# Two edits to a two-layer attention trunk: the mixing ratio of projections and attention in its second layer, and the position bias of the compression on Pool and DVE

## The chip, the cores and the metric

The kernel runs on one core of a Trainium2 chip. Its engines are TensorE (PE; its weight loads are listed as PEld), VectorE (DVE), ScalarE (ACT) and GpSimd (POOL); SyncE (SP) issues the DMAs. The metric is the device time of one execution in microseconds, taken as the median of several runs. In the rows, L1265 is line 1265 of the kernel before; busy times are in us.

## What is computed

Two layers over 1024 tokens of width 1024, in float32. The first has an attention with the 256 best keys for each query (a) and a sliding-window attention (b). The second, with which the change deals, has a three-part attention (c) and a latent attention (d). Cut to what matters:

```python
def nsa_compress(z, pe, w1, w2):                 # keys and values of (c), blocks of 32 tokens, step 16
    ch = z.reshape(bsz, seq // 16, 16, 2, 64)
    blocks = concatenate([ch[:, :-1], ch[:, 1:]], axis=2) + pe[None, None, :, None, :]
    flat = blocks.transpose(0, 1, 3, 2, 4).reshape(bsz, 63, 2, 32 * 64)
    return silu(flat @ w1) @ w2                  # w1: 2048 x 128

def layer_cd(x, ...):
    y = rms_norm(x, norm_g) @ w_in               # all projections: qc kc vc ks vs kw vw gc zc cq ckv kr zd
    kc, vc = nsa_compress(kc, ...), nsa_compress(vc, ...)
    oc = nsa_attention(...)                      # compressed keys + all keys of blocks + window of 512
    q  = rms_norm(cq) @ d_w_uq                   # 8 heads x (64 + 32)
    kv = rms_norm(ckv) @ d_w_ukv                 # 8 heads x (64 keys + 64 values)
    od = mla_attention(...)                      # causal over all keys
    return x + concatenate([oc * silu(zc), od * silu(zd)]) @ w_out
```

Because the bias `pe` is added ahead of the linear map, `(z + pe) @ w1` is `z @ w1` plus one vector of 128 numbers for the keys and one for the values.

## The kernel before

The tokens lie in 8 tiles of 128. Every projection is a chunk of up to 280 columns (`chunk`, `fill_gen`, L480 to L543): for each tile it accumulates 8 x 3 matmuls in a bank of PSUM (`pp`, two banks; weights and input are split into a high and a low part, so three products) and hands the bank to a `post` function, which copies it out and mostly posts a chain of further steps (norm, rotation, transposes through the three buffers of `psT`).

The order is written by a planner, `Lanes`. A main generator (the attention) and a fill generator (the projections) yield costs in planner units; after each main step, `Lanes.run` (L153) takes fill steps until the fill's sum reaches `ratio` times the main's sum. A unit of scores costs heads x 2 x max(107, 0.42 x keys), a block of transposes 110 and a block of value products 87 for each 128x128; a quarter of a projection tile costs 6 x max(107, 0.42 x columns). Posted chains advance by one step with each of these steps. The result is a program order; the framework then places each engine's instructions by a timeline of its own in which the program order is the priority, so that an instruction that is ready may go ahead of earlier ones that wait, as far as buffers allow; buffers of a pool come in program order.

Layer two runs as follows. `FO` holds the last projection of layer one and then the chunks `ks kc kw qc0 zc0 zc1 cq qc1 zd0 zd1 ck` (FOO, L57). When `kc` is through, `compress()` (L1254) is posted: for keys (n = 0) and then values (n = 1) it forms the bias, as 16 matmuls of one column against the 16 slices of `w1` (L1265), then the hidden layer (L1276) and the second map (L1291). When the first queries are there, `L.run(attn_gen(c_jobs(0) + c_jobs(1)), FC, CR)` (L1792) runs the three-part attention: for each half of the heads (g) eight query tiles in the order CO, each as compressed, full and window unit. It is filled with the rest of `FO` and behind it `d_prologue` (L1616): it closes the pool of projection weights, opens the one of the last attention in the same space, loads and splits that attention's weights (`small_w`), makes the keys of its first four heads (`d_keys`, eight tiles in pairs) and up to two queries (`next_query`). The chunk `cq` is held back until the first half of the heads is done (`gate`, L1485), since it takes the buffers of that half's keys. What of the fill is left when the attention has been planned, up to the last keys, follows at L1793. Then the values of the last attention are made (L1802; their buffers are those of the three-part attention's values), and the last attention runs with its own fill, `d_fill`, and with `wout_gen`, which loads and splits the output weights. The chunk `ck` (keys' latent) is 160 columns wide; its chain ends with the copy `krs` (L1465).

Names in rows: `pt` probabilities, `hp`/`ht` their transposed halves, `hl` their split for a transposing DMA, `po` the values' sum, `kcs` the compressed keys, `qs` queries, `kd`, `qhl`, `qrs` keys and queries of the last attention, `whq`, `whkv` its weights, `rs_y` reciprocal roots, `gnope` its gains.

Of the kernel before, what the change touches and what calls it, by code (L numbers as in the profile page):

```python
# [10 lines left out]
F32 = mybir.dt.float32  # L11
# [7 lines left out]
OP = mybir.AluOpType  # L19
AX = mybir.AxisListType  # L20
PSUM = bass.MemoryType.PSUM

P = 128
# [21 lines left out]
QB = 3  # L45
TR = 1.4
TA = 0.65
CR = 0.88
DR = 0.8
WB = 2  # L50
WP = 2
# [19 lines left out]
PTB = 3  # L71
# [113 lines left out]
def trunk(ctx: ExitStack, tc: tile.TileContext, A, out):  # L185
    nc = tc.nc
    V, S, G, T = nc.vector, nc.scalar, nc.gpsimd, nc.tensor
# [4 lines left out]
    wk = ctx.enter_context(tc.tile_pool(name="wk", bufs=2))  # L192
# [25 lines left out]
    half = cst.tile([P, 16], F32, name="half")  # L218
# [140 lines left out]
    def tps():  # L359
        return psT.tile([P, 4, P], F32, name="psT")  # L360
# [727 lines left out]
    for c in tk:  # L1088
        m += c
        L.tick()  # L1090
        while f < TR * m and c is not None:
            c = next(FA)
# [161 lines left out]
    def compress():  # L1254
        for n in range(2):
            w1 = B["w1"][n]
            zT = B["zT"][n]
            pe = cp.tile([P, 16], F32, name="pe")
            nc.sync.dma_start(pe, A["c_cmp_pe"][0, n].rearrange("(a b) d -> (b d) a", b=2))
            w2 = cp.tile([P, 64], F32, name="w2")  # L1260
            nc.sync.dma_start(w2, A["c_cmp_w2"][0, n])
            yield from L.take_in("psT", PTC)
            ph = tps().rearrange("p a n -> p (a n)")
            for a in range(16):
                T.matmul(ph[:, 0:1], w1[:, a], pe[:, a:a + 1], start=a == 0, stop=a == 15)  # L1265
            bias = cp.tile([P, 2], F32, name="bias", bufs=2)
            V.tensor_copy(bias[:, 0:1], ph[:, 0:1])
            L.give("psT")
            V.tensor_scalar(bias[:, 1:2], bias[:, 0:1], 0.5, None, op0=OP.mult)
            yield  # L1270
# [4 lines left out]
            for a in range(16):  # L1275
                T.matmul(p2[:, :, 0:NCMP], w1[:, a], zT[:, :, 2 * a:2 * a + 16 * (NCMP - 1) + 1:16],  # L1276
                         start=a == 0, stop=a == 15)
# [196 lines left out]
    def cchunk(*a, **k):  # L1474
        return chunk(*a, src="x1T", **{"tiles": AO[1], **k})

    c_kc = cchunk(wcd, CD["kc"], CD["ks"], kc_post, pre=kc_pre,
                 post_all=lambda: L.post(compress()))
    c_ks = cchunk(wcd, CD["ks"], CD["kw"], ksq, pre=ksp)
    c_kw = cchunk(wcd, CD["kw"], CD["zc"], kw_post, pre=kwp, post_all=kw_all)  # L1480
# [13 lines left out]
    def c_jobs(g):  # L1494
        return [job_c(i, g, k) for i in CO[g] for k in range(3)]
# [138 lines left out]
    def fo_then():  # L1634
        yield from FO
        yield from d_prologue()
# [154 lines left out]
    FC = fo_then()  # L1791
    L.run(attn_gen(c_jobs(0) + c_jobs(1)), FC, CR)  # L1792
    while ("kd", 0, 6) not in L.done:  # L1793
# [74 lines left out]
```

## Time and profile before

| | us |
|---|---|
| median of three runs (1494.69 to 1501.79) | 1495.83 |
| the profiled execution, its own time | 1506.33 |
| its span, first to last instruction | 1504.5 |
| PE / PEld busy | 1331.0 / 1221.2 |
| DVE / ACT / POOL busy | 1004.0 / 939.7 / 908.6 |
| start of `compress`'s bias matmuls (keys, values) | 740.9, 765.4 |
| first scores against compressed keys | 814.2 |
| first scores of the last attention | 1231.2 |

Matmuls overlap, and the ends in the rows are modelled, so the sum of their durations is more than the time in which PE worked; a busy PE says that it had something to do, not that it ran at its peak. PEclk and the granted clock give TensorE's clock as a share of 2.4 GHz.

### The profile page before, as it was taken

What the parts mean: (1) busy time and instruction counts of PE and PEld (TensorE: products, weight loads), DVE (VectorE), ACT (ScalarE), POOL (GpSimd) and SP (SyncE); (2) the same over time, 40 slices, a digit from 0 to 9 for tenths busy, and PEclk for the clock granted to TensorE, in tenths of its full rate; (3) what the DMA queues carried; (4) which work ended last, traced back from release to release, by engine and by line L of the source; (5) the groups of instructions that cost most, each with busy time, mean ns of one, the idle gap of its engine ahead of it and who ended that gap; (6) DMA issues with size and microseconds to landing.
All of it is one profiled execution on the core that took longest, in us unless ns stands there. A gap on an engine that the chain in (4) does not pass through costs nothing. (4 is left out here: it accounts for less than half of the span.)

```text
span 1504.5 us, 33785 instructions
## 1 busy us (share of the span) xinstructions
PE 1331.0 (88%) x12132; PEld 1221.2 (81%) x12132; DVE 1004.0 (67%) x2788; ACT 939.7 (62%) x2683; POOL 908.6 (60%) x1196
## 2 busy tenths in 40 slices
PE   5998899888248999999999998899998868889998
PEld 5998888788247788999999997699996757778887
DVE  5397887787887966244225757756668889986552
ACT  5354588877658866144424677866768869866531
POOL 6798648896467486227349353365244799875440
PEclk9999999898659999999999999999999879999999
DMA  6311264322041244132311253312334414334442
GB/s 205 91 32 31 68 134 92 81 49 69 12 109 59 83 108 131 44 120 70 75 33 53 75 106 76 64 46 62 78 61 71 117 56 98 82 86 102 128 128 79
DMA packets 208936, 122.81 MB, mean 82 GB/s; under 512 B 141696, under 2 KB 193664, under 8 KB 208768
## 3 DMA queue, kind: packets, MB, share of 16 engines
q1 hardware_dynamic: 208768, 120.65, 32.0%
q8 instruction: 95, 1.56, 0.4%
q14 instruction: 73, 0.60, 0.1%
HBM read 67.65 MB, written 23.07 MB: 60 GB/s over the span
## 5 line engine op out<-in xcount | busy, mean ns | idle before, releaser
L520 PE MATMUL pp<-whi,Rh 128*128 128x256 f32 (+4 forms) x1648 | 483.2, 294 | 22.7 <-ACT sq L454 6.6
L521 PE MATMUL pp<-wlo,Rh 128*128 128x256 f32 (+4 forms) x1648 | 477.6, 290 | 1.1 <-POOL wlo L477 1.1
L522 PE MATMUL pp<-whi,Rl 128*128 128x256 f32 (+4 forms) x1648 | 478.2, 290 | 0.0
L520 PEld LDWEIGHTS pp<-whi,Rh 128*128 128x128 f32 x1648 | 319.3, 194 | 28.4 <-ACT sq L454 7.7
L521 PEld LDWEIGHTS pp<-wlo,Rh 128*128 128x128 f32 x1648 | 319.4, 194 | 3.1 <-POOL wlo L477 1.5
L522 PEld LDWEIGHTS pp<-whi,Rl 128*128 128x128 f32 x1648 | 319.4, 194 | 1.1
L689 ACT ACTIVATE pt<-pt,nm 128x256 f32<-128x256 f32 (+8 forms) x384 | 244.9, 640 | 5.5
L477 POOL TENSOR_TENSOR wlo<-wraw,whi 128x256 fp32r<-128x256 f32 (+4 forms) x208 | 163.5, 795 | 129.2 <-ACT whi L476 123.0
L711 POOL TENSOR_TENSOR hl<-pt,hl 128x512 f16<-128x512 f32 x114 | 136.9, 1203 | 110.1 <-ACT hl L710 83.6
L476 ACT ACTIVATE whi<-wraw 128x256 fp32r<-128x256 f32 (+4 forms) x208 | 83.2, 416 | 135.6 <-DMA wraw<-in_cd_w_in 48.2
L730 PE MATMUL psT<-identf,pt 128*128 128x128 f32 x800 | 144.7, 286 | 12.4 <-ACT pt L689 6.0
L733 ACT ACTIVATE hp<-psT 128x512 f16<-128x512 f32 (+3 forms) x241 | 109.0, 462 | 59.9 <-PE psT L730 55.5
L683 DVE CUSTOM_DVE_ANT_0 pt<-psS,mk 128x512 f32<-128x512 f32 (+4 forms) x208 | 107.0, 522 | 47.9 <-PE psS L680 37.1
L734 DVE TENSOR_TENSOR hp<-psT,hp 128x512 f16<-128x512 f32 (+3 forms) x241 | 123.3, 521 | 23.1 <-ACT hp L733 21.7
L303 POOL TENSOR_TENSOR rs_y<-rs_v,half 128x8 f32<-128x8 f32 (+3 forms) x102 | 122.5, 1203 | 3.9
L730 PEld LDWEIGHTS psT<-identf,pt 128*128 128x128 f32 x800 | 95.5, 144 | 26.2 <-ACT pt L689 13.7
L660 PEld LDWEIGHTS <-hp 128*128 128x128 f16 x800 | 73.4, 98 | 26.0 <-ACT hp L733 7.6
L687 ACT ACTIVATE nm<-nm 128x1 f32<-128x1 f32 (+2 forms) x208 | 42.0, 203 | 83.6 <-DVE nm L683 82.4
L663 PEld LDWEIGHTS <-hp 128*128 128x128 f16 x800 | 72.1, 98 | 23.8 <-DVE hp L734 14.7
L661 PEld LDWEIGHTS <-hp 128*128 128x128 f16 x800 | 73.7, 99 | 2.7 <-issue 1.8
L710 ACT ACTIVATE hl<-pt 128x512 f16<-128x512 f32 x114 | 71.0, 628 | 7.6 <-DMA ht<-hl 4.9
L689 ACT ACTIVATION_READ_ACCUMULATOR pt<-pt,nm 128x1 f32 x384 | 73.5, 191 | 0.0
(317 smaller groups left out, 3641.8 us busy)
## 6 DMA issues: line engine op xcount, KB each, us to landing
wraw<-in_cd_w_in SPq DMA_DIRECT2D x72, 128.0 KB, 2.1
wraw<-in_ab_w_in SPq DMA_DIRECT2D x56, 128.0 KB, 2.5
xs<-in_x SPq DMA_DIRECT2D x8, 512.0 KB, 6.0
od<-mx SPq DMA_DIRECT2D x32, 128.0 KB, 1.9
wraw<-in_ab_w_out SPq DMA_DIRECT2D x32, 128.0 KB, 2.2
x<-in_x SPq DMA_DIRECT2D x8, 512.0 KB, 4.7
mo<-od SPq DMA_DIRECT2D x16, 256.0 KB, 3.0
nz<-zdr SPq DMA_DIRECT2D x16, 256.0 KB, 3.0
```

Of the source, the lines that this page charges most:

```text
L303: G.tensor_tensor(y, v, half[:w, :n], OP.pow)
L476: S.activation(hi[:, :o], raw[:, :o], AF.Copy)
L477: G.tensor_tensor(lo[:, :o], raw[:, :o], hi[:, :o].bitcast(F32), OP.subtract)
L520: T.matmul(ps, xh, hi[:, :n], start=q == 0 and k == 0, stop=False)
L521: T.matmul(ps, xh, lo[:, :n], start=False, stop=False)
L522: T.matmul(ps, xl, hi[:, :n], start=False, stop=q == 3 and k == 1)
L683: V.tensor_tensor_reduce(pt[:, j * nk + c:j * nk + c + w], ps[:, at:at + w], mask(c, w), -1.0, first, op0=OP.add, op1=OP.min, accum_out=low)
L689: S.activation(pt[:, j * nk:(j + 1) * nk], pt[:, j * nk:(j + 1) * nk], AF.Exp, scale=-1.0, bias=nm[:, h:h + 1], accum_out=sm[:, h:h + 1])
L711: (V if way[-1] == "d" else G).tensor_tensor(hl[:, w:], pt[:, o:o + w], hl[:, :w], OP.subtract)
L730: T.transpose(pT[:, a], pt[:, o:o + P], identf)
L733: S.activation(ph, pT[:, :n], AF.Copy)
L734: V.tensor_tensor(pl, pT[:, :n], ph, OP.subtract)
```

## The change

Two things. The ratio CR of the planner, with which the three-part attention is filled, goes from 0.88 to 1.0. And the bias of the compression is formed in another way: POOL multiplies the 16 slices of `w1` (128 rows each, 128 columns) by the matching columns of `pe`, eight slices at a time into a buffer of the pool's `pt`; DVE sums over the eight; two matmuls against a column of -0.5 (`half`, which was there) sum over the 128 rows, and the copy out of PSUM becomes a multiply by -2.0. Two `yield`s are added, one behind each sum.

```diff
-CR = 0.88
+CR = 1.0
...
+            u = wk.tile([P, 256], F32, name="pesum", tag="mx", bufs=3)
+            for a in range(0, 16, 8):
+                t = wk.tile([P, 1024], F32, name="pt", bufs=PTB).rearrange("p (a c) -> p a c", a=8)
+                G.tensor_tensor(t, w1[:, a:a + 8], pe[:, a:a + 8, None].to_broadcast([P, 8, P]), OP.mult)
+                V.tensor_reduce(u[:, 16 * a:16 * a + P], t.rearrange("p a c -> p c a"), AX.X, OP.add)
+                yield
             yield from L.take_in("psT", PTC)
             ph = tps().rearrange("p a n -> p (a n)")
-            for a in range(16):
-                T.matmul(ph[:, 0:1], w1[:, a], pe[:, a:a + 1], start=a == 0, stop=a == 15)
+            for a in range(2):
+                T.matmul(ph[:, 0:1], u[:, a * P:(a + 1) * P], half[:, 0:1], start=a == 0, stop=a == 1)
             bias = cp.tile([P, 2], F32, name="bias", bufs=2)
-            V.tensor_copy(bias[:, 0:1], ph[:, 0:1])
+            V.tensor_scalar(bias[:, 0:1], ph[:, 0:1], -2.0, None, op0=OP.mult)
```

## Rows read from the trace of the kernel before

**Rows 1.** the page: its span, and part 1, the busy time of each engine

```profile
span 1504.5 us, 33785 instructions
PE 1331.0 (88%) x12132; PEld 1221.2 (81%) x12132; DVE 1004.0 (67%) x2788; ACT 939.7 (62%) x2683; POOL 908.6 (60%) x1196
```

**Rows 2.** stretches: length; PE, PEld, DVE, ACT, POOL busy; granted clock; DMA share; GB/s

```profile
725.00:815.00 90.00, 90.00 (x675) 88.88 (x674) 29.66 (x75) 33.59 (x105) 47.55 (x73) 0.92 0.16 38
905.00:978.00 73.00, 63.90 (x761) 51.27 (x758) 55.29 (x217) 58.25 (x178) 25.67 (x26) 0.98 0.36 72
1120.00:1155.00 35.00, 29.27 (x352) 23.82 (x351) 25.93 (x99) 25.37 (x80) 11.68 (x14) 1.00 0.44 66
1177.00:1193.00 16.00, 13.59 (x89) 10.02 (x88) 11.97 (x44) 15.38 (x50) 10.47 (x18) 0.72 0.51 123
1193.00:1207.00 14.00, 10.28 (x136) 9.08 (x136) 12.49 (x33) 11.09 (x36) 12.37 (x12) 0.96 0.49 123
1207.00:1231.00 24.00, 13.13 (x67) 10.52 (x63) 19.50 (x55) 16.48 (x48) 21.56 (x23) 0.73 0.15 52
1231.00:1350.00 119.00, 100.48 (x913) 85.24 (x913) 104.15 (x272) 95.73 (x263) 106.94 (x125) 0.94 0.35 87
1350.00:1500.00 150.00, 149.86 (x1155) 125.18 (x1154) 81.05 (x209) 65.56 (x169) 60.36 (x70) 1.00 0.43 111
```

**Rows 3.** timeline of PE, compress: start, us, engine, line, operation, count

```profile
740.94 4.33 PE L1265 MATMUL psT<-pe,w 128*128 128x1 f32 x32
745.13 5.47 PE L1276 MATMUL psT<-zT,w 128*128 128x126 f32 x24
765.36 4.99 PE L1265 MATMUL psT<-pe,w 128*128 128x1 f32 x32
777.49 1.88 PE L1276 MATMUL psT<-zT,w 128*128 128x126 f32 x8
```

**Rows 4.** stretches as in rows 2, around the two bursts of bias matmuls

```profile
740.00:755.00 15.00, 15.00 (x96) 14.93 (x95) 2.04 (x7) 3.59 (x11) 3.11 (x5) 0.77 0.31 58
765.00:775.00 10.00, 10.00 (x58) 9.81 (x57) 1.87 (x7) 1.62 (x7) 5.82 (x10) 0.66 0.00 0
```

**Rows 5.** lines: ns min/median/max, first to last start; nearest to the added operations

```profile
L1678 POOL TENSOR_TENSOR ydup<-nz,gnope x16: 1267/1286/1325, 1226.7 to 1449.3; 128x512 f32<-128x512 f32 x16
L595 DVE TENSOR_REDUCE vs_m<-pt x5: 1207/1220/1221, 44.6 to 1202.2; 128x1 f32<-128x1024 f32 x5
```

**Rows 6.** projections' matmuls of L520 alone: length, PE, PEld busy (count), clock, DMA

```profile
905.00:978.00 73.00, 2.90 (x10) 1.89 (x10) 0.98 0.36 72
1120.00:1155.00 35.00, 1.84 (x7) 1.14 (x6) 1.00 0.44 66
```

**Rows 7.** timeline of PE: first scores of three units against the compressed keys

```profile
913.38 0.39 PE L680 MATMUL psS<-kcs,qs 128*128 128x64 f32 x2
968.46 0.41 PE L680 MATMUL psS<-kcs,qs 128*128 128x64 f32 x2 [0.19 <-DVE nm L683]
1121.23 0.39 PE L680 MATMUL psS<-kcs,qs 128*128 128x64 f32 x2
1167.55 0.34 PE L680 MATMUL psS<-kcs,qs 128*128 128x64 f32 x2
```

**Rows 8.** lines at the change of attention, columns as rows 5

```profile
L1465 ACT ACTIVATE krs<-psT x8: 255/279/314, 1155.2 to 1205.8; 128x128 fp32r<-128x128 f32 x8
L1521 SPq DMA_DIRECT2D wraw<-in_d_w_uq x4: 328/380/529, 1176.9 to 1268.9; - x4
L1356 DVE TENSOR_TENSOR cacc<-po,rs x48: 392/424/426, 833.9 to 1207.8; 128x256 f32<-128x256 f32 x48
L680 PE MATMUL psS<-kd,qhl x192: 222/368/793, 1231.2 to 1472.1; 128*128 128x512 f32 x72, 128*128 128x256 f32 x48, 128*128 128x320 f32 x32, 128*128 128x384 f32 x24
L1557 ACT ACTIVATE kd<-psT x28: 363/382/387, 1207.8 to 1340.9; 64x256 fp32r<-64x256 f32 x28
```

**Rows 9.** timeline of POOL at the keys of the last attention

```profile
1198.93 1.66 POOL L303 TENSOR_TENSOR rs_y<-rs_v,half 128x8 f32<-128x8 f32 x1
```

## The prediction

> **What bounds the kernel now.** I read the page first, then the stretches, then single lines. TensorE (PE) is busy 88% of the span and DVE 67% [rows 1], but that average hides stages with different limits. Around the compression (725 to 815 us) PE has no idle time at all while DVE, ACT and POOL stand at a third to a half of the 90 us: this stage is bound by PE, and a microsecond of matmul taken out there is a microsecond of the span, as long as nothing else takes its place [rows 2]. From 905 to 978 us the three-part attention runs without projections: 10 matmuls of L520 in 73 us [rows 6], PE busy 63.9 of 73 [rows 2]. From 1120 to 1155 it is the same picture, 7 matmuls of L520 [rows 6], PE 29.3 of 35 [rows 2]. Then comes the change from the three-part attention to the last one: from 1177 to 1231 us PE is busy 13.6 of 16, 10.3 of 14 and 13.1 of 24 us, with a mean granted clock of 0.72, 0.96 and 0.73, while POOL goes up to 21.6 of 24 [rows 2]. The last attention's first 119 us have POOL at 106.9 and DVE at 104.2; from 1350 us on PE is full again [rows 2]. So two places have something to give: matmuls of the compression, and the hole at the change of attention.
>
> **The bias.** Two bursts of 32 matmul records go (16 matmuls in two passes, once for each of keys and values). The first occupies PE from 740.94 to 745.13 us, when the next burst begins: 4.2 us; the second takes 4.99 [rows 3]. Two matmuls for each are added, 8 records at 4.33/32 = 0.135 us: 1.1 us. Net: 8.1 us less of PE in a stage that PE bounds. Added on POOL: four products of 128x1024; the nearest row has 1286 ns for 128x512 with a broadcast operand [rows 5], so 2.57 us each, 10.3 in all. Added on DVE: four sums over 1024 elements; the nearest row, a reduce of 1024 elements, takes 1.22 us [rows 5]. Here the elements are read with a stride and 128 sums leave instead of one; no row shows that, so I bound it by once and twice the row (below the row nothing speaks for a gain) and take 1.22. Cover: POOL is idle 42 of the 90 us and DVE 60 [rows 2], and PE has projections to issue in the meantime, since the two added yields put two more projection quarters ahead of the bias matmul. If that cover is missing, PE waits for product, product, sum, 2 x 2.57 + 1.22 = 6.4 us per half, 12.7 for both; the bias would then cost 12.7 - 8.1 = 4.6 us. Behind the waiting bias matmul are queued the compression's own matmuls and the projections; behind POOL's products are queued the normalisations of the key projections. I take no exposure: **-8.1 us**, bounds -8.1 and +4.6. The added multiply by -2.0 replaces a copy and costs the same.
>
> **The clock there.** The granted clock averages 0.77 over the 15 us that hold the first burst and 0.66 over 10 us that hold the second [rows 4], so 15 x 0.23 + 10 x 0.34 = 6.8 us of full clock are withheld; a stretch runs at 2.4 or 1.2 GHz, and it falls while or just after PE issues one-column matmuls. What would come back if the bursts go? The compression's matmuls run mostly in the slow part: 24 records in 5.47 us behind the first burst, 0.228 each; 8 records after the second dip take 1.88, 0.235 each [rows 3]. They don't gain from the higher clock. I count 0. By the Trainium skill, "TensorE: Matmul & The Clock Gate", section "Terms", the penalty of a throttled stretch is its time multiplied by the share of pulses withheld; that is an estimate of 6.8 us here, against the row's 0, and it is a rival below.
>
> **The ratio.** CR only sets how many projection units the planner interleaves per attention unit. I added up its costs from the code. The attention is worth 158.0 thousand units (K) at either ratio. At 0.88 the first 160-column projection (ck) has its quarters from 141.8K on, its first tile is finished at 143.7K, and nine quarters, the weights, the keys and two queries of the last attention come after all attention work. At 1.0 the first tile is finished at 135.6K, the last at 153.7K; the eight key tiles stand at 154.3K to 156.7K and two queries behind them, beside the last unit (tile 5, window part). What is this worth? ck's matmuls run ahead of their place until its buffers are full; the copy that ends its chain (krs) first runs at 1155.2 us [rows 8], because its PSUM buffer comes in program order behind the attention's. So the hole from 1120 to 1155 ends when the attention reaches ck's first tile, and that is now 143.7 - 135.6 = 8.1K earlier. The attention's own rate comes from the first scores against the compressed keys: 913.38 us at 31.7K to 968.46 us at 67.2K, nearly without projections, 1.55 us per K; 1121.23 at 118.9K to 1167.55 at 144.2K, 1.83 [rows 7]. 8.1K are 12.6 to 14.8 us; I take 12.6, the stretch without projections being nearest to this hole. From there everything hangs on one chain: end of ck, the DMA of the query weights at 1176.9 us, which reuses ck's weight buffers, the keys, the queries, and the last attention's first scores at 1231.2 [rows 8]. These four weight DMAs, the projections' weight loads and the gate stores all move earlier in SP's queue, ahead of some transposing DMAs of the attention; none of them is added. On PE the keys are 48 records, at the bias records' 0.135 us 6.5 us, and nearly fit into the 2.4 + 3.7 = 6.1 us of idle time from 1177 to 1207 [rows 2]. On ACT they don't: it is busy 15.4 of the 16 us from 1177 on [rows 2], and the keys' 16 copies and squares at 0.38 each, the nearest row [rows 8], are 6.1 us in front of the attention's exponentials. Half of that, 3.0, I let through to the end. Net **-9.6 us**; bounds: 0, if the first scores don't move, and -23.4, when they come right behind the last attention's sum at 1207.8 [rows 8].
>
> **The gate in the middle.** The cq projection can't begin before the first half of the heads is through (75.2K). At 0.88 the last quarter before it stands at 63.9K, at 1.0 at 56.4K: by plan 7.5K more of attention without projections, 7.5 x 1.55 = 11.6 us, in which PE idles (73 - 63.9)/73 = 12.5% [rows 2]: **+1.5 us**. The debt is then paid in a longer run of projections alone, which keeps PE full and costs nothing. Bounds 0 (in the trace projections have run ahead and are gone by 905 us anyway) and 1.5.
>
> **The sum.** The profiled execution took 1506.33 us (span 1504.5, 1.8 around it). -8.1 - 9.6 + 1.5 = -16.2 gives 1490.1. The runs' median is 1495.83, 0.9930 of it, and none of the three was as slow as the profiled one; scaled, 1490.1 is **1480 us**.
>
> **Rivals.**
> - *The ratio doesn't set the order.* By plan projections go on beside the attention up to 63.9K; in the trace they end at 905 us, when the attention stands near 29K [rows 6, 7]. PE takes whatever is ready, and buffers, not CR, set the place. Then only the bias counts: -8.1 + 1.5 = -6.6, 1499.7, scaled 1489. Against it: ck's chain does follow program order.
> - *POOL's queue in front of the attention's tail (slower).* Each pair of key tiles needs 1.66 for its reciprocal roots [rows 9] and 1.27 for the gain, four pairs 11.7; two queries at least 1.66 + 0.6 + 2 x 1.27 = 4.8 each, 9.6. That is 21.3 us, in order on POOL, ahead of the subtractions that the last units' transposes wait for. POOL has 5.5 + 1.6 = 7.2 us free from 1177 to 1207 [rows 2]; from there on each microsecond delays the attention's end: 14.1, and ACT's 3.0, with no earlier start of the last attention. -8.1 + 1.5 + 17.1 = +10.5: 1516.8, scaled 1506. Against it: most of this work becomes ready only after 1193 now, and half of it may still sort itself behind.
> - *The whole hole closes.* -23.4 in place of -9.6: -30.0, 1476.3, scaled 1466. For it: POOL and DVE, nearly full from 1231 to 1350 [rows 2], get rid of work too.
> - *The clock comes back.* The 6.8 us withheld in the compression return on top: -23.0, 1483.3, scaled 1473. For it: PE is full there. Against it: the records' equal length in and out of the dip. (This is what the skill's rule above would make of it.)
>
> **How the numbers follow.** Chances: forecast 0.45, ratio without effect 0.22, POOL in front 0.12, whole hole 0.10, clock 0.11. A measurement of this kernel can tell about 0.5% (7.5 us) from no change, so faster means under 1488.4 and slower over 1503.3. Faster: 0.41 of the forecast's 0.45, 0.05 of the second case, all of the last two, 0.67; slower: nearly all of POOL's case, 0.11; within: 0.22. The range from 1464 to 1498 holds the forecast, the ratio without effect with part of the bias exposed, the clock and most of the whole hole; it leaves out POOL's case and the lower end.
>
> **What would show it.** In the profile after: no burst of one-column matmuls, and POOL's four products and DVE's four sums beside full PE, with no idle PE before the two bias matmuls; the granted clock there tells the clock rival. krs's first copy about 12 us earlier against the attention's tile 5, the query weights' DMA likewise, the keys' matmuls before the attention's end and the first scores of the last attention close behind it. If krs moves but the first scores don't, the hole was POOL's; if krs doesn't move, the ratio was without effect. The prediction fails if the scheduler, given other priorities, shuffles the stages after the gate so that PE waits in new places; no row can price that.

## The result and the profile after the change

The changed kernel takes 1511.27 us (median of six runs, 1506.34 to 1518.97), the kernel before beside it on the same chip 1496.88: ratio 1.0097, 95% interval 1.0079 to 1.0115. The forecast was 1480 us and faster; it is slower by about 1%.

The page of the changed kernel, its span and part 1:

```profile
span 1504.6 us, 33663 instructions
PE 1326.5 (88%) x12076; PEld 1210.3 (80%) x12076; DVE 1013.0 (67%) x2792; ACT 934.6 (62%) x2683; POOL 915.0 (61%) x1200
```

Against [rows 1] the totals say almost nothing: PE 4.5 us less, DVE 9.0 and POOL 6.4 more, the same span. That the spans agree is an accident. The trace of before that the prediction rests on is of an execution 10 us above its median; the changed kernel's is of the fastest of its six. Two more executions of the unchanged kernel were profiled below, with spans of 1494.5 and 1498.8 us, and the stages are compared with these.

Stretches of the changed kernel (length; PE, PEld, DVE, ACT, POOL busy; granted clock; DMA share; GB/s), which answer to [rows 2]:

```profile
725.00:815.00 90.00, 86.15 (x638) 83.95 (x638) 35.89 (x96) 33.97 (x117) 61.77 (x89) 0.96 0.17 45
1177.00:1193.00 16.00, 12.32 (x82) 10.34 (x81) 15.52 (x38) 11.99 (x45) 13.92 (x14) 0.71 0.36 98
1193.00:1207.00 14.00, 10.25 (x100) 7.66 (x99) 12.65 (x42) 11.49 (x34) 12.02 (x12) 0.97 0.26 57
1207.00:1231.00 24.00, 19.73 (x148) 14.24 (x147) 18.96 (x53) 17.69 (x44) 17.96 (x22) 0.79 0.38 94
1231.00:1350.00 119.00, 95.26 (x893) 82.03 (x894) 97.97 (x261) 90.94 (x258) 97.58 (x113) 0.90 0.33 82
1350.00:1500.00 150.00, 149.86 (x1145) 125.16 (x1144) 82.57 (x209) 64.95 (x169) 62.41 (x73) 1.00 0.42 110
```

Two things stand out. PE, which had no idle time around the compression, now has 3.85 us of it. And in front of the last attention DVE is full, 15.52 of 16 us, where it had 11.97 [rows 2]; from 1231 to 1350 us every engine has less work than before, since the last attention begins earlier here. The lines that answer to [rows 8] (duration in ns min/median/max, first to last start):

```profile
L1472 ACT ACTIVATE krs<-psT x8: 256/277/413, 1139.6 to 1182.9; 128x128 fp32r<-128x128 f32 x8
L1528 SPq DMA_DIRECT2D wraw<-in_d_w_uq x4: 328/330/570, 1155.6 to 1252.7; - x4
L1363 DVE TENSOR_TENSOR cacc<-po,rs x48: 395/421/425, 820.3 to 1227.6; 128x256 f32<-128x256 f32 x48
L680 PE MATMUL psS<-kd,qhl x192: 272/378/796, 1214.3 to 1472.1; 128*128 128x512 f32 x72, 128*128 128x256 f32 x48, 128*128 128x320 f32 x32, 128*128 128x384 f32 x24
L1564 ACT ACTIVATE kd<-psT x28: 361/381/392, 1191.1 to 1342.1; 64x256 fp32r<-64x256 f32 x28
```

Everything that was to move earlier did: ck's first copy (krs) from 1155.2 to 1139.6, the query weights' load from 1176.9 to 1155.6, the keys from 1207.8 to 1191.1, the last attention's first scores from 1231.2 to 1214.3. But the three-part attention's last sum (cacc) went from 1207.8 to 1227.6.

The stages of ten traces. K is the end of the last copy of kc and S the end of the attention's last sum; the others are starts: the first score against the compressed keys (C), the first projection matmul after the stretch in which the attention runs alone (G, the gate), the last attention's first score (D), the first output matmul (O); then the span's end. All in us.

| kernel | K | K to C | C to G | G to S | G to D | D to O | O to end |
|---|---|---|---|---|---|---|---|
| before, second trace | 733.0 | 73.2 | 168.6 | 223.6 | 246.1 | 116.1 | 157.5 |
| before, third trace | 734.6 | 73.4 | 170.5 | 224.4 | 246.8 | 115.9 | 157.6 |
| after | 730.0 | 70.8 | 178.5 | 248.7 | 235.0 | 133.8 | 156.5 |
| new bias only | 732.8 | 69.9 | 176.9 | 225.6 | 248.8 | 116.6 | 158.0 |
| new bias, keys only | 732.7 | 70.1 | 168.1 | 222.9 | 247.2 | 118.3 | 156.5 |
| new bias, values only | 730.4 | 74.0 | 174.3 | 223.9 | 245.5 | 118.8 | 156.4 |
| bias of two slices | 732.1 | 66.8 | 173.8 | 221.8 | 244.8 | 112.4 | 156.4 |
| bias by a chain on DVE | 732.4 | 69.0 | 173.1 | 222.7 | 245.9 | 113.5 | 157.2 |
| ratio 1.0 only | 737.6 | 75.8 | 170.0 | 249.3 | 235.3 | 133.4 | 156.7 |
| ratio 1.0, keys behind | 732.4 | 73.7 | 169.9 | 233.0 | 246.8 | 115.8 | 155.8 |

So the change loses in two places: 5 to 8 us from K to G, which is the bias, and some 6 us from G to O (368.8 against 362.2 and 362.7), where the first scores come 11 us earlier and the first output 18 us later behind them. Counted from the gate, which the first trace of before reaches 4.5 us later than the changed kernel (983.8 against 979.3), ck's first copy comes 9 to 11 us earlier than in the three traces of before, the first scores 11 to 12 us earlier, and the last sum 24 to 25 us later.

### The profile page after: what moved, and what is told of

It is laid out like the page before. It is cut to its first block, busy times and chain, and to the rows that moved or that the text cites. A ratio compares the mean times of both kernels' runs of the same rounds, so it can differ in the third digit from the quotient of the medians.

```text
span 1504.6 us, 33663 instructions
## 1 busy us (share of the span) xinstructions
PE 1326.5 (88%) x12076; PEld 1210.3 (80%) x12076; DVE 1013.0 (67%) x2792; ACT 934.6 (62%) x2683; POOL 915.0 (61%) x1200
## 4 chain that ended last, share of the span: by engine, by line
PE 39%; DVE 15%; ACT 10%; DMA 7%; POOL 5%; issue 5%; SPq 0%; ACTq 0%; POOLq 0%; DVEq 0%
PE pp L520 6%; PE psS L680 6%; PE pp L522 6%; PE pp L521 5%; ACT pt L689 3%; PE psT L730 3%; DVE pt L683 3%; PE pp L1758 2%; PE pp L1760 2%; PE pp L1759 2%; DMA ht<-hl 2%; DMA wraw<-in_cd_w_in 2%; ACT junka L904 1%; DVE junk L908 1%; PE po L663 1%
## 5 line engine op out<-in xcount | busy, mean ns | idle before, releaser
L520 PE MATMUL pp<-whi,Rh 128*128 128x256 f32 (+4 forms) x1648 | 481.9, 293 | 24.4 <-ACT sq L454 6.7
L520 PEld LDWEIGHTS pp<-whi,Rh 128*128 128x128 f32 x1648 | 316.9, 193 | 31.6 <-ACT sq L454 7.9
L689 ACT ACTIVATE pt<-pt,nm 128x256 f32<-128x256 f32 (+8 forms) x384 | 244.5, 641 | 4.8
L683 DVE CUSTOM_DVE_ANT_0 pt<-psS,mk 128x512 f32<-128x512 f32 (+4 forms) x208 | 106.9, 522 | 49.2 <-PE psS L680 35.0
L660 PEld LDWEIGHTS <-hp 128*128 128x128 f16 x800 | 74.3, 99 | 25.5 <-issue 6.5
L663 PEld LDWEIGHTS <-hp 128*128 128x128 f16 x800 | 73.3, 99 | 22.6 <-DVE hp L734 11.9
L661 PEld LDWEIGHTS <-hp 128*128 128x128 f16 x800 | 74.7, 100 | 3.1 <-issue 2.1
```

Of the source, the lines that this page charges most:

```text
L520: T.matmul(ps, xh, hi[:, :n], start=q == 0 and k == 0, stop=False)
L683: V.tensor_tensor_reduce(pt[:, j * nk + c:j * nk + c + w], ps[:, at:at + w], mask(c, w), -1.0, first, op0=OP.add, op1=OP.min, accum_out=low)
L689: S.activation(pt[:, j * nk:(j + 1) * nk], pt[:, j * nk:(j + 1) * nk], AF.Exp, scale=-1.0, bias=nm[:, h:h + 1], accum_out=sm[:, h:h + 1])
```

## The experiments

**The unchanged kernel again.**

> The kernel before, unchanged, for a second trace: the first one took 1506 us, 10 more than the median of its runs, so its stages don't stand for them. If layer one is what varies, its last kc copy comes 6 to 10 us earlier than the 738.3 of the first trace, and from there to the end it takes the same 766 us. If the stages behind it vary, the 766 us become 756 to 760.

> As before_again: a third trace of the unchanged kernel, so that the spread of each stage from execution to execution is known (layer one, compression, three-part attention, last attention), beside the differences between kernels of 4 to 14 us.

1496.26 and 1500.56 us, spans 1494.5 and 1498.8. Single profiled executions of one program differ by several us (about half of the 10 us between the first trace and the second lies ahead of K, 738.3 against 733.0); so a verdict below goes by the medians, and a trace is only asked where time is spent.

**One part alone.** The new bias at ratio 0.88, then the old bias at ratio 1.0 (`CR = 1.0`):

> The new bias at the old ratio (0.88). The forecast's own term: 8.1 us less of TensorE in a stretch that it bounds, so 1489 us, 0.5% faster than before. The trace after starts the three-part attention 5.1 us earlier than before, counted from the last copy of the kc projection (70.8 us from one to the other, against 75.9), so 1492 is as likely. Rival, that any change of the program order reshuffles the attention behind it: 1500 or more.

1507.83 us, ratio 1.0079 (1.0055 to 1.0102).

> The old bias at the ratio 1.0. If the ratio carries the whole loss and the bias its gain, this is the slowest of the four, 1516 to 1520 us (after, 1511, plus the 5 to 8 us of the bias). If the loss comes from the new bias or from both together, 1497, as before, or the 1487 of the forecast's -9.6.

1506.05 us, ratio 1.0067 (1.0043 to 1.0092), which neither side of its expectation named. Each part alone makes the kernel slower. Together they cost less than their sum (0.97% against 1.46%).

**Is it only that the order was disturbed?** The kernel before with two empty steps in each half of the compression, and with a ratio of 0.87:

```diff
             w2 = cp.tile([P, 64], F32, name="w2")
             nc.sync.dma_start(w2, A["c_cmp_w2"][0, n])
+            yield
+            yield
```

> The kernel before with two empty steps at the place where the new bias has its two yields: no instruction is added or taken away, only the program order of the compression against the projections shifts by two steps. Theory of the order (the kernel before has an order that happens to fit, and any shift of it costs): 1503 to 1508, as with the new bias alone. Theory of the work (POOL's products, DVE's sums or what they wait for cost the time): 1496, as before.

1500.83 us, ratio 1.0013 (0.9995 to 1.0031).

```diff
-CR = 0.88
+CR = 0.87
```

> The kernel before at the ratio 0.87, a step of 0.01 the other way: by the planner's sums the keys and queries stay behind the attention, and at its end only 1.6 thousand units (three quarters of a projection) have moved. Theory of the order: 1501 to 1508, like the ratio 1.0 alone (1506). Theory that the projections' lead or the keys in front of the tail make the loss: 1495 to 1498.

1499.68 us, ratio 1.0018 (1.0002 to 1.0033). These two shifts of the order cost some 0.15%, which doesn't explain 0.7%. For shifts of this size the theory fell; larger ones were not tried.

**Which half of the bias.** `if n == 0` (keys) or `if n == 1` (values) takes the new way, the other half keeps the 16 matmuls:

> Bias formed in the new way for the keys' half only (values keep the 16 matmuls), ratio 0.88. Theory (the loss sits in the values' half, where POOL's products wait 9.7 us for the second load of w1 and DVE's two sums of 1.97 us stand ahead of copies that free the projections' banks): the keys' half alone gains up to its 3 to 4 us of PE, 1491 to 1497. Rival (each half costs the same half of the new bias's 12 us): 1501 to 1504.

1494.40 us, ratio 0.9993 (0.9978 to 1.0008).

> Bias formed in the new way for the values' half only (keys keep the 16 matmuls), ratio 0.88. Theory (loss in the values' half): 1504 to 1511. Rival (half of it in each): 1501 to 1504. If this one comes at 1497 or under and the keys' half over 1504, the loss sits in the keys' half.

1504.64 us, ratio 1.0055 (1.0033 to 1.0076). The loss sits in the values' half; the keys' half neither costs nor gains measurably. (The halves add up to 0.48%, against 0.79% for both together; with these intervals the difference is not shown.) The timeline of POOL there, the second trace of before first, then the kernel with the values' half alone (start, us, engine, line, operation, out<-in, count, idle time before it and what ended it):

```profile
741.89 1.42 POOL L477 TENSOR_TENSOR wlo<-wraw,whi 128x256 fp32r<-128x256 f32 x2 [3.57 <-ACT whi L476]
752.19 0.34 POOL L302 TENSOR_SCALAR rs_v<-ss 64x2 f32<-64x2 f32 x2 [8.88 <-DVE ss L1304]
```

```profile
739.51 0.73 POOL L477 TENSOR_TENSOR wlo<-wraw,whi 128x256 fp32r<-128x256 f32 x1
751.03 3.76 POOL L1266 TENSOR_TENSOR pt<-w,pe 128x1024 f32<-128x1024 f32 x2 [10.79 <-DMA w<-in_c_cmp_w]
754.75 0.34 POOL L302 TENSOR_SCALAR rs_v<-ss 64x2 f32<-64x2 f32 x2
```

POOL is idle before either, but not for the same reason. The values' `w1` takes over a buffer that the keys' hidden layer still reads: its DMA waits for PE. SP's waits from 735 to 760 us in the kernel with the values' half (engine, line, what it waited for: us in total, times, longest):

```profile
SPq L1224 <- PE psT L1290: 2.7, 1, 2.7
```

It lands at 751 us, just when the compressed keys' own chain is ready to go on, and the two products stand in front of that chain: it starts 24.4 us after K, where it started 19.2 us after it. Then DVE's two sums, of 2.05 and 1.85 us, run from 752.96 to 756.91 us, and the short copy (vlw) that helps to free a projection's bank starts only behind them, at 757.15, though its input was there at 754.24. The waits of PE from 735 to 800 us, same kernel:

```profile
PE pp L520 <- ACT gat L1355: 1.5, 2, 1.2
PE psT L1305 <- issue: 1.3, 1, 1.3
PE psT L567 <- DVE vs_m L1336: 0.9, 1, 0.9
```

ACT, whose copy the first line names, had itself been idle for 3.29 us until DVE's vlw. For the other two waits no link to the new work is shown ("issue" means that the profile shows nothing that was waited for). The sum of these three is the idle time that PE shows in the stretch around the compression (second trace of before, values' half, and the kernel with two slices, below):

```profile
725.00:815.00 90.00, 90.00 (x699) 88.86 (x698) 30.11 (x84) 31.75 (x101) 55.38 (x83) 0.96 0.17 43
725.00:815.00 90.00, 86.27 (x639) 84.26 (x638) 32.13 (x88) 31.25 (x105) 58.42 (x85) 0.94 0.17 42
725.00:815.00 90.00, 89.19 (x689) 87.78 (x689) 35.73 (x102) 37.40 (x125) 60.72 (x90) 1.00 0.20 50
```

3.73 us of PE's time are lost, as much as the values' 32 matmuls occupied in the second trace (3.73 us; 4.99 in [rows 3]). The projections that PE did not do meanwhile come later: 384 projection matmuls are recorded between K and C in each trace of before and 359 in this one, and 25 more behind C.

**Which engine's work.** The values' half without DVE's sums, and without POOL's products (both cut to the line that matters):

```diff
-                    V.tensor_reduce(u[:, 16 * a:16 * a + P], t.rearrange("p a c -> p c a"), AX.X, OP.add)
+                    u.append(t)
```

> New bias for the values' half only, with POOL's two products but without DVE's two sums (the matmuls take the first slice of each product; the rest of the sum is left out). Theory D (DVE's two sums of 1.97 us hold up the copies that free the projections' banks): 1495 to 1500. Theory P (POOL's products, which start only with the second load of w1, delay the key chain queued behind them and the second hidden layer): 1503 to 1507.

1502.43 us, ratio 1.0027 (1.0006 to 1.0047).

```diff
-                    G.tensor_tensor(t, w1[:, a:a + 8], pe[:, a:a + 8, None].to_broadcast([P, 8, P]), OP.mult)
-                    V.tensor_reduce(u[:, 16 * a:16 * a + P], t.rearrange("p a c -> p c a"), AX.X, OP.add)
+                    V.tensor_reduce(u[:, 16 * a:16 * a + P], w1[:, a:a + 8].rearrange("p a c -> p c a"), AX.X, OP.add)
```

> New bias for the values' half only, without POOL's products (DVE sums w1 itself; the multiplication by the bias is left out). Theory P: 1495 to 1500. Theory D: 1503 to 1507. If this one and the kernel without the sums are both at 1503 or over, neither engine's work but the longer way to the second hidden layer costs.

1494.96 us, ratio 0.9987 (0.9965 to 1.0010). Neither expectation holds whole; theory P comes nearer. Without the products the loss of 0.55% is gone, so most of it needs POOL; without the sums about half is gone, though that interval overlaps the one with the sums. The chain product, product, sum behind the load costs, POOL's part of it most clearly. PE's idle time from 725 to 815 us does not measure the loss: it is 3.28 us without the products, where nothing is lost, and 2.47 without the sums, where 0.27% is. Nor do postponed projections alone: with the two empty steps 364 stand between K and C, for 0.13%. The loss goes with the whole way from K to the gate: 248.3 us with the values' half, 246.9 without the sums, 244.5 without the products, 241.8 and 243.9 before.

**What the removed matmuls are worth.** First the bias left out altogether:

```diff
-            for a in range(16):
-                T.matmul(ph[:, 0:1], w1[:, a], pe[:, a:a + 1], start=a == 0, stop=a == 15)
...
-            V.tensor_copy(bias[:, 0:1], ph[:, 0:1])
+            V.memset(bias[:, 0:1], 0.0)
```

> The kernel before with the position bias left out altogether (part of the computation is missing): no one-column matmuls, no products on POOL, no sums on DVE, ratio 0.88. Theory (the removed matmuls are worth their PE time, and the new way of forming the bias gives it back elsewhere): about 8 us under the kernel before, 1487 to 1491. Rival (a stage between the compression and the gate is not set by PE, so matmuls taken out of the compression are worth nothing at the end): 1494 to 1500.

1502.47 us, ratio 1.0032 (1.0011 to 1.0053). It answers nothing: the order of PE's matmuls departs from that of before already in layer one, at 521 us, where the other kernels depart at 722 us or later, and K stands at 740.4 us. From K to G it takes 237.4 us, the shortest of all. So the matmuls were cut down instead, to 2 of 16 slices:

> The kernel before with the bias formed from 2 of the 16 slices only, by the old one-column matmuls (the other 14 are left out), ratio 0.88; PE's order ahead of the compression stays as before. Theory (the removed matmuls are worth their PE time, about 7 of the 8.1 us): 1489 to 1493. Rival (matmuls taken out of the compression are worth nothing at the end, as the attention behind it takes the time back): 1495 to 1500.

1493.10 us, ratio 0.9959 (0.9937 to 0.9981): 6.1 us gained (0.41% of 1497.88; 2.8 to 9.4 by the interval). By [rows 3] 14 of 16 matmuls occupy 8.0 us (4.2 and 4.99 us, times 14/16). But the bursts differ from trace to trace: in the second trace of before they are shorter,

```profile
735.72 3.63 PE L1265 MATMUL psT<-pe,w 128*128 128x1 f32 x32
759.33 3.73 PE L1265 MATMUL psT<-pe,w 128*128 128x1 f32 x32
```

and 3.49 and 3.59 us pass from the start of each to the next matmul, the same in the third trace. 14/16 of that are 6.2 us, so PE's time there is worth about itself, as the forecast said. In the trace the gain is not where it was made: K to C is 6.5 us shorter, C to G about 4 longer, and D to O 3.6 shorter again. So a C that comes earlier is partly given back up to the gate in any case, without a wait on POOL.

**The way to the last attention.** The changed kernel and the kernel at ratio 1.0 with the old bias, both with the last attention's weights, keys and queries planned behind the three-part attention instead of beside it:

```diff
+    L.run(attn_gen(c_jobs(0) + c_jobs(1)), FO, CR)
     FC = fo_then()
-    L.run(attn_gen(c_jobs(0) + c_jobs(1)), FC, CR)
```

> As after, but the last attention's weights, keys and queries are planned behind the three-part attention, as at 0.88; the projections stay at 1.0. Theory of the tail: keys and queries on DVE and ACT in front of the attention's last two units move its end from 1208 to 1228 us; without them the end returns to some 1208 and the time to 1500 or less. Theory of the middle: the loss arises before the last units (at the fourth query tile of the second half of the heads the trace after has lost what it had gained), so this stays at 1507 to 1515.

1506.77 us, ratio 1.0069 (1.0045 to 1.0092), against 1.0097 (1.0079 to 1.0115) with the keys beside; the intervals overlap. The last sum went back to 1210 us, as the theory of the tail had it, but the time did not go to 1500: about the loss of the new bias alone (1.0079) is left.

> Old bias, ratio 1.0, but weights, keys and queries of the last attention planned behind the three-part attention, so that only its projections (ck among them) move. Theory (the keys in front of the attention's tail carry the ratio's loss): 1495 to 1500. Rival (the projections moved forward, ck above all, carry it): 1503 to 1508.

1497.73 us, ratio 1.0013 (0.9997 to 1.0029), against 1.0067. With the old bias the last attention's weights, keys and queries together carry nearly the whole loss of the ratio (below "the keys"; which of them was not tested); the projections alone, ck among them, are free to move and worth nothing. The last sum comes 9 us later than before in that kernel (G to S 233.0), and that costs nothing. What the keys do there, by stretches (columns as above; ratio 1.0 with keys behind, then the changed kernel):

```profile
1177.00:1207.00 30.00, 23.11 (x221) 18.82 (x221) 23.46 (x67) 22.02 (x63) 25.70 (x23) 0.82 0.47 110
1207.00:1231.00 24.00, 16.09 (x77) 12.93 (x76) 19.83 (x54) 17.93 (x52) 17.92 (x22) 0.66 0.19 61
```

```profile
1177.00:1207.00 30.00, 22.58 (x181) 18.00 (x179) 28.18 (x79) 23.48 (x76) 25.94 (x26) 0.83 0.32 79
1207.00:1231.00 24.00, 19.73 (x148) 14.24 (x147) 18.96 (x53) 17.69 (x44) 17.96 (x22) 0.79 0.38 94
```

DVE goes from 23.46 to 28.18 of 30 us; ACT and POOL hardly change. (DVE has 25.32 in the changed kernel with the keys behind, 26.84 at ratio 1.0 with the old bias and the keys beside.) Among the costliest groups of DVE in the changed kernel from 1176 to 1230 us are these (line, names, shapes, count, busy us, mean ns, idle before):

```profile
L683 DVE CUSTOM_DVE_ANT_0 pt<-psS,mk 128x512 f32<-128x512 f32 (+1 forms) x12 | 7.4, 619 | 0.8 <-PE psS L680 0.7
L683 DVE CUSTOM_DVE_ANT_0 pt<-psS,mk,nm 128x256 f32<-128x256 f32 (+2 forms) x12 | 7.0, 587 | 0.2
L1565 DVE TENSOR_TENSOR kd<-psT,kd 64x256 fp32r<-64x256 f32 x16 | 6.7, 422 | 1.6 <-ACT kd L1564 1.2
L1548 DVE TENSOR_TENSOR nz<-nz,rs_y 128x512 f32<-128x512 f32 x4 | 3.9, 972 | 0.0
L1542 DVE TENSOR_REDUCE ss<-sq 128x8 f32<-128x512 f32 x4 | 2.7, 672 | 0.0
```

The keys' split (L1565), normalisation (L1548) and sums of squares (L1542) are 13.3 us of DVE, beside the attention's masks and maxima (L683). That DVE delays the last sum is read from these shares; no run separates it from the work of the other engines and the loads that moved along. The values of the last attention need the buffers of the three-part attention's values, and so the end of its last value products (1226.8 us), just ahead of its last sum. PE's timeline shows the price, value matmuls of L1575 in the changed kernel:

```profile
1194.94 0.36 PE L1575 MATMUL pp<-whkv,Rh 128*128 128x256 f32 x1
1197.68 0.38 PE L1575 MATMUL pp<-whkv,Rh 128*128 128x256 f32 x1
1228.50 0.28 PE L1575 MATMUL pp<-whkv,Rh 128*128 128x256 f32 x1
```

and DVE's, at its end:

```profile
1227.56 0.42 DVE L1363 TENSOR_TENSOR cacc<-po,rs 128x256 f32<-128x256 f32 x1
1227.89 0.34 DVE L603 SCALAR_TENSOR_TENSOR vdl<-pp,vs_e,vdh 128x128 f16<-128x128 f32 x1
```

The products for two tiles of values are made early, take both projection banks, and wait: no matmul of L1575, nor any other into these banks, runs for 31 us, and the next follows the start of the attention's last sum within a microsecond. The first scores, 11 us early, bring nothing, since values and further queries follow them from this point: D to O is 133.8 us in place of 116. From S to O, on the other hand, it takes 120.1 us here and 119.4 at ratio 1.0 alone, where it takes 138.6 before and 129.6 with the keys behind: this fits a first output that follows the last sum in the first two and the first scores in the others, so that a later last sum costs only from the point where it becomes the later of the two.

**Ratio by halves.** The changed kernel with 0.88 up to the gate and 1.0 from there:

```diff
-    L.run(attn_gen(c_jobs(0) + c_jobs(1)), FC, CR)
+    L.run(attn_gen(c_jobs(0) + c_jobs(1)), FC, lambda l: 1.0 if ('cg', 0) in l.done else 0.88)
```

> As after, but with the ratio 0.88 until the first half of the heads is done and 1.0 from there on (the plan's sum is kept, only the rate changes). Theory of the middle: the first half's lead of the projections costs about 9 us (from the attention's start to the first scores of its last tile before the gate, the two traces differ by 13.4 - 4.3 = 9.1 us), so 1502. Theory of the tail: the tail is as in after, so 1508 to 1512.

1507.51 us, ratio 1.0070 (1.0043 to 1.0097), from four runs. The time lies nearer to the theory of the tail (1508 to 1512) than to that of the middle (1502), but the new bias alone (1.0079) and the whole change (1.0097) are both inside or at the interval. It tells nothing apart.

**Both suspects undone.** The changed kernel with the values' bias by the old matmuls and the keys behind:

> The changed kernel with its two suspects undone: the values' bias by the old matmuls, and the last attention's weights, keys and queries planned behind the three-part attention; ratio 1.0 and the keys' new bias stay. Theory (these two carry the whole loss): 1492 to 1499. Rival (new bias and ratio together cost in another place): 1503 to 1508.

1495.41 us, ratio 0.9985 (0.9965 to 1.0005). Undoing these two takes away the whole loss, while ratio 1.0 and the keys' new bias stay.

**A way to form the bias without POOL and without long sums.** Against the changed kernel, cut to the sums:

```diff
-            for a in range(0, 16, 8):
-                t = wk.tile([P, 1024], F32, name="pt", bufs=PTB).rearrange("p (a c) -> p a c", a=8)
-                G.tensor_tensor(t, w1[:, a:a + 8], pe[:, a:a + 8, None].to_broadcast([P, 8, P]), OP.mult)
-                V.tensor_reduce(u[:, 16 * a:16 * a + P], t.rearrange("p a c -> p c a"), AX.X, OP.add)
-                yield
+            V.tensor_scalar(u, w1[:, 0], pe[:, 0:1], None, op0=OP.mult)
+            for a in range(1, 16):
+                V.scalar_tensor_tensor(u, w1[:, a], pe[:, a:a + 1], u, op0=OP.mult, op1=OP.add)
+                if a % 8 == 7:
+                    yield
```

> Bias for both halves by 16 chained multiply-adds on DVE (128x128 each, an estimate of 0.34 us from the nearest row, L603, 5.4 us for a half) and one matmul; no work for it on POOL, no long sum; ratio 0.88. Theory (POOL's products ahead of the key chain and the long sums ahead of the bank copies cost, the freed matmuls are worth 6 us): 1490 to 1495. Rival (any way that starts only when the values' w1 has landed delays the second hidden layer and gives the gain back): 1498 to 1504.

1493.13 us, ratio 0.9976 (0.9957 to 0.9996), and so a little faster than both kernels, though less than 0.5%. DVE's line for it:

```profile
L1266 DVE SCALAR_TENSOR_TENSOR pesum<-w,pe,pesum x30: 325/352/1136, 718.2 to 761.3; 128x128 f32<-128x128 f32 x30
```

It takes 5.6 us of DVE for a half (15 at 0.352 and a first product at 0.286), more than the two sums' 4.0, but other instructions go in between, and POOL's key chain runs ahead. It still waits for the load, and PE is idle 2.76 us from 725 to 815.

> The same bias as chained multiply-adds on DVE, with ratio 1.0 and the last attention's weights, keys and queries planned behind the three-part attention. Theory (the projections' ratio alone is neutral): within 3 us of the kernel with the chain at 0.88, 1489 to 1496. Rival (the two together cost): 1500 to 1506.

1500.82 us, ratio 1.0015 (0.9997 to 1.0033). The rival is nearer: 0.39% more than the chain at 0.88, where with the 16 matmuls the same ratio and plan cost 0.13%. In its trace the time goes from D to O, 121.9 us in place of 113.5; I have no cause for that.

## Why the prediction was wrong

**The bias, -8.1.** The step that failed is "I take no exposure". The cover was read from shares of 90 us: POOL idle 42, DVE 60. That time was there, but the values' `w1` was not: it is loaded only once the keys' hidden layer has been through PE, and it lands where the old one-column matmuls could still wait (they ran at 765 [rows 3]) and the longer new chain cannot. The prediction named the key projections' normalisations behind POOL's products and priced them at nothing. Measured for the bias alone: +11.9 us, outside both bounds. The upper one, +4.6, counted only PE's bare wait, up to 12.7 us. With the new bias alone PE is idle for 3.95 us from 725 to 815 us, far less than that, and the rest of the loss stands behind it, between C and the gate (176.9 us, 168.6 and 170.5 before), for which the sum had no term. Sizes: POOL's product took 1.90 us (2.57 forecast, from half the width with a broadcast), DVE's strided sum 1.98 (1.22 taken, twice that as its bound). The removed matmuls were taken from a trace in which they ran long: 9.2 us there, 7.1 in the second and third traces; the added ones, 1.1 in the forecast, take 0.7 in the changed kernel. So the gain to be had was 6.4, not 8.1. With these sizes the other half of the step stands: with two slices, 6.1 us were gained at the end for the 6.2 us of matmuls cut away. The postponed projections go with the longer way from C to the gate; part of it comes with an earlier C in any case, as with two slices; the rest is not settled.

**The ratio, -9.6.** The mechanism moved as forecast: D came 11 us earlier after the gate, for the 12.6 forecast. What failed is the second half of the step, "half of that, 3.0, I let through": only ACT's and PE's share of the keys was costed. Measured for the ratio alone: +10.2 us. DVE's share, 13.3 us up to the attention's end, was not in the sum at all, and the last sum came 16 us later than with the keys behind (G to S 248.7 against 233.0). The sentence "From there everything hangs on one chain" was the error beneath it: the last attention needs the values too, and they hang on the buffers of the attention that had just been delayed. The rival with POOL's queue in front of the attention's tail had the place and nearly the delay of the last sum (17 us). That its 1506 us is the time of the ratio alone is luck: it contains -8.1 for the bias and counts the delay in full. By the shares its engine was wrong, POOL being at 25.94 of 30 us where it is 25.70 with the keys behind.

**The gate, +1.5.** C to G is 170.0 us with ratio 1.0 alone, 168.6 and 170.5 before: no more than 1.5 either way, as bounded.

**The clock.** Without most of the one-column matmuls the granted clock stays at its upper level from 740 to 755 us; it was 0.77 there in the first trace [rows 4] and 0.89 in the second (second trace of before, then two slices):

```profile
740.00:755.00 15.00, 15.00 (x99) 14.66 (x98) 2.45 (x8) 3.30 (x13) 4.23 (x9) 0.89 0.41 92
740.00:755.00 15.00, 15.00 (x101) 14.56 (x101) 3.35 (x10) 4.20 (x17) 5.94 (x13) 1.00 0.33 90
```

Nothing comes back for the matmuls behind the bursts: K to C is 6.4 to 6.6 us shorter, about the 6.2 us of the removed matmuls themselves. In the first trace 24 of the 126-column matmuls run in 5.47 us [rows 3] while the granted clock is 0.50, one every 0.22 us; with two slices, at 1.00, one starts every 0.21 us:

```profile
738.34 7.04 PE L1276 MATMUL psT<-zT,w 128*128 128x126 f32 x32
```

So the count of 0 was right for these, and the rival falls. The one-column matmuls themselves do run slower in the dip. In the first trace they start every 0.112 us at a granted clock of 1.00 and every 0.213 us at 0.50 (medians); the matmuls of L1265 alone, in a stretch of either kind (length, PE and PEld busy, clock, DMA share, GB/s):

```profile
741.00:743.60 2.60, 2.60 (x25) 2.60 (x25) 1.00 0.23 61
767.80:770.00 2.20, 2.20 (x11) 2.20 (x12) 0.50 0.00 0
```

That is why [rows 3] has them at 9.2 us and the other two traces at 7.1: the forecast had part of this rival in its own term without seeing it. By the Trainium skill, "TensorE: Matmul & The Clock Gate", section "Terms", an estimate of 6.8 us would have come back on top; the trace doesn't agree, since the 126-column matmuls run as fast at either level and some 2 us of the first trace's one-column time is all that the dips account for in these rows.

**The scaling** of the profiled 1506.33 to the median was right: two more traces of before gave 1494.5 and 1498.8 us. **The range** to 1498 left out 1511 because only POOL's case, with a chance of 0.12, was given a slower result; the bias's own bound of +4.6 had no case. Each part alone was outside the range.

What stays open: why the effects don't add (0.79% and 0.67% give 0.97%; moving the keys behind gives back 0.54% with the old bias and 0.28% with the new, the latter within the intervals); what makes the way from C to the gate longer; and which of the pieces that moved with the keys delays the last sum. Loading the values' `w1` earlier, into a buffer of its own, was not tried.

## What to carry to other kernels

Idle time of an engine is cover only where its input is already there: look up when the operand of a moved instruction lands, and what is queued behind it on that engine. Work that is brought forward beside another stage's tail is paid for on every engine that it touches, and if a later step needs that tail's buffers, the delayed tail sets that step's start as soon as it is the last thing waited for. Where a sum must stand in a queue that frees banks for TensorE, short pieces of it may cost less than their total suggests: 16 short steps on DVE gained 0.24% where product and long sum lost 0.79%, though here POOL's products went with the long sums. And read the price of what is removed from more than one trace.

## What the runs showed of the hardware

A product of 128x1024 elements with a broadcast operand took 1.90 us on POOL. A sum on DVE over 8 strided elements for each of 128 results took 1.98 us, 1.6 times a sum of the same 1024 elements to one result (1.22) [rows 5]. A chained multiply-add of 128x128 on DVE took 0.35 us in the median. From 740 to 755 us the granted clock is 0.77 and 0.89 in two traces with the bursts of one-column matmuls and 1.00 with an eighth of them. One-column matmuls start every 0.112 us at a granted clock of 1.00 and every 0.213 us at 0.50; the 126-column ones behind them start every 0.21 to 0.22 us either way.
